# One more gate through half-size products, and a shorter score loop in attention

## The chip, the cores and the metric

The kernel runs on one core of a Trainium2 chip. A core has a matrix engine (TensorE, PE in the profile; its weight loads stand as PEld), a vector engine (VectorE, DVE), an activation engine (ScalarE, ACT), a general engine (GpSimd, POOL) and an engine whose queue issues nearly all transfers (SyncE, SP). They run side by side and wait for each other by semaphores. Matrix products land in PSUM, eight banks of 512 float32 numbers on each of 128 partitions; everything else is held in SBUF. The metric is the time of one execution on the device in microseconds, as a median of runs.

## The reference

One layer on 1024 latent tokens and 256 context tokens of width 1024. A normalised, modulated input `h` goes through one wide projection, whose columns feed two branches and their gates:

```python
pl = project(modulate(x, sh_x, sc_x), w_in[layer])
...
s1 = jnp.einsum('bhqd,bhkd->bhqk', qb1, k1).astype(jnp.float32) * scale
s2 = jnp.einsum('bhqd,bhkd->bhqk', qb2, k2).astype(jnp.float32) * scale
a = jax.nn.softmax(s1, axis=-1) - lam * jax.nn.softmax(s2, axis=-1)
return jnp.einsum('bhqk,bhkv->bhqv', a.astype(v.dtype), v)
...
a = merge_heads(rms_norm(o_gla) * gla_gain) * jax.nn.silu(gla_gate)
b = merge_heads(rms_norm(o_diff) * diff_gain * (1 - lam_init)) * jax.nn.silu(diff_gate)
y = jax.nn.sigmoid(m_gla) * (a @ w_br_gla) + jax.nn.sigmoid(m_diff) * (b @ w_br_diff)
return y @ w_out
```

Branch A is a gated linear attention (`o_gla`); branch B is differential attention over 8 heads: each query has two softmaxes ("components") over 1280 keys, and the second, times a number `lam`, is taken from the first. `m_gla` and `m_diff` are the two merge gates, each a 1024 x 1024 by 1024 x 1024 product of `h` with columns of `w_in`.

## The kernel before

A planner in Python writes the order of every engine's instructions. Each piece of work is a generator with a priority; the `Driver` (lines 46 to 187) keeps an estimated clock for each engine, resumes the generator that is due with the lowest priority number, and adds the instruction's estimated cost. `acq` and `rel` hand out buffers of a tag (line 235: tag, pool, number of buffers), an `Event` passes a dependency on. What comes out is a fixed order for each engine; on the chip an engine waits where an operand is late. All compute instructions are issued at two helper lines: 201 for ACT, DVE and POOL, 349 for matmuls (375 for transposes), so the profile tells them apart by tile names.

Every float32 product is three passes of rounded halves (`mm3`, line 354): high by high, high by low, low by high.

The stages, in order of time:

1. Input, norms, and the products for the linear attention's keys and queries.
2. Groups of paired products (`pairs`, line 1097; `BY7`, line 907): a product of two 2 x 2 block matrices is made with seven half-size products (`p1` to `p7`) and sums of blocks. Four groups so far: the two value projections (five tiles of 128 tokens a half) and the two branch gates (four tiles, `dg` and `gg`). The sums of blocks of `h` (`sums`, line 909) are stored to DRAM once and loaded by each group, 16 loads a group; the sums of the weights are made on DVE (`pair_weights`, line 943).
3. "Late" products (keys and queries of differential attention, six slices of the first merge gate) run on TensorE while the linear attention (`gla_head`, line 1499) goes through all engines.
4. Differential attention: 8 heads x 8 query tiles = 64 tiles of 128 queries.
5. The product of branch B and the output product, again by seven half-size products (`diff`, `phase_c`).

Attention, which the change touches most: `att_scores` (line 1940) makes a tile's scores in one PSUM area `s5` of five banks: 1280 columns of component 0, 1280 of component 1. Bank 2 holds the end of the one and the start of the other, the "tail" (two pieces of 256 columns, `TAIL`). Three tokens guard the area: `s0`, `s1`, and `st` for the shared bank, released after both exponentials. For each tile DVE takes three maxima (`att_max`, line 1991: 1024 columns of component 0, the tail for both, 1024 of component 1), two minima join them (the maxima are negated), and ACT makes two exponentials over 1280 columns that read PSUM and sum as they go (`att_exp`, line 1998). `att_mix` (line 2018) joins the two on DVE: `E0 + cf * E1`. `att_tr` (line 2039) transposes the mix in ten pieces of 128 columns on TensorE, `split2` (line 2120) makes the halves on ACT, POOL and DVE, and `att_av` (line 2068) multiplies by the values, two tiles ("a pair") at a time. `att_fin` (line 2143) normalises a pair's output: copy, transpose, sum of squares, product with the gate from DRAM, power -0.5 on POOL, scaling, transpose back, store.

The order of scores (S), transposes (T) and value products (A) on TensorE is written out by hand (`att_order`, line 1915): scores run three to four tiles ahead of transposes. Whatever TensorE time is left is given to `fill` (line 2194), priority 9, the last of all: half tiles of 24 matmuls. Its list is two slices of the first merge gate, all eight of the second, and eight of `a @ w_br_gla`; slice by slice, halves of tokens in turn. `PACE` (line 2107) holds the i-th half tile back until query tile `1.3 * i` has its scores. PSUM in attention: five banks of scores, two banks `b1` for transposes, value products and the finish, one bank `mb` for the filler.

## Time and profile before

| | |
|---|---|
| time, median of 3 runs (lowest to highest) | 1619.05 us (1618.73 to 1619.51) |
| the profiled execution | span 1614.1 us from the first to the last instruction; its own time isn't given apart from the median, 4.95 us over the span |
| granted TensorE clock, mean | 1.000 |
| busy share of PE, PEld, DVE, ACT, POOL | 99%, 82%, 76%, 52%, 39% |
| DMA | 331.16 MB, mean 205 GB/s |
| attention, first score to last exponential | 898.8 to 1428.6 us |

A row of a group reads: line, engine, operation, output tile <- input tiles, shapes, count | busy microseconds, mean nanoseconds of one | idle time of the engine ahead of them, and who ended it. Matmuls are pipelined: the duration of one is longer than the distance to the next. A row of the timeline has start and length in microseconds, engine, operation, tiles and count, then in brackets the idle time before it. A row of the chain has start, length, engine, output tile and line.

### The profile page before, as it was taken

What the parts mean: (1) busy time and instruction counts of PE and PEld (TensorE: products, weight loads), DVE (VectorE), ACT (ScalarE), POOL (GpSimd) and SP (SyncE); (2) the same over time, 40 slices, a digit from 0 to 9 for tenths busy, and PEclk for the clock granted to TensorE, in tenths of its full rate; (3) what the DMA queues carried; (4) which work ended last, traced back from release to release, by engine and by line L of the source; (5) the groups of instructions that cost most, each with busy time, mean ns of one, the idle gap of its engine ahead of it and who ended that gap; (6) DMA issues with size and microseconds to landing.
All of it is one profiled execution on the core that took longest, in us unless ns stands there. A gap on an engine that the chain in (4) does not pass through costs nothing.

```text
span 1614.1 us, 24349 instructions
## 1 busy us (share of the span) xinstructions
PE 1591.4 (99%) x8229; PEld 1328.1 (82%) x8229; DVE 1224.4 (76%) x2118; ACT 835.7 (52%) x1720; POOL 634.3 (39%) x663
## 2 busy tenths in 40 slices
PE   8999999999999999999999999999999999999999
PEld 3788888888888888888888788888888888888887
DVE  4787945676777779767677688878778888888994
ACT  4776523435343454555535566665665666656331
POOL 1500000001415667535564256656765666560000
PEclk9999999999999999999999999999999999999999
DMA  8576996998878367564645944545587545347662
GB/s 305 201 257 239 329 304 232 344 331 295 278 238 281 116 194 235 167 212 118 189 118 158 253 121 121 151 129 151 150 264 218 159 137 150 111 155 285 204 206 100
DMA packets 259565, 331.16 MB, mean 205 GB/s; under 512 B 22600, under 2 KB 160752, under 8 KB 259440
## 3 DMA queue, kind: packets, MB, share of 16 engines
q1 hardware_dynamic: 259440, 329.60, 63.8%
q8 instruction: 65, 1.06, 0.3%
q14 instruction: 60, 0.49, 0.1%
HBM read 225.20 MB, written 104.33 MB: 204 GB/s over the span
## 4 chain that ended last, share of the span: by engine, by line
PE 89%; DVE 4%; issue 2%; DMA 2%; ACT 1%; POOL 1%; SPq 0%; ACTq 0%; DVEq 0%; POOLq 0%
PE mm L349 30%; PE mb L349 11%; PE s L349 8%; PE mc L349 7%; PE b L349 6%; PE tp L349 5%; PE gt L349 5%; PE b L375 5%; PE go L349 4%; PE gs L349 4%; PE mz L349 2%; PE tp L375 2%; DVE sm L201 1%; POOL at L201 1%; DMA w<-in_w_ada 1%
## 5 line engine op out<-in xcount | busy, mean ns | idle before, releaser
L349 PE MATMUL mm<-w,h 128*128 128x512 f32 x912 | 231.0, 400 | 0.0
L349 PE MATMUL mb<-h,wt 128*128 128x512 f32 x840 | 223.0, 400 | 0.0
L201 DVE TENSOR_REDUCE sm<-s 128x1 f32<-128x1024 f32 (+1 forms) x192 | 193.3, 1037 | 10.7 <-PE s L349 6.6
L201 ACT ACTIVATE e<-s,sm 128x1280 f32<-128x1280 f32 x128 | 169.3, 1329 | 54.4 <-DVE sm L201 51.2
L349 PEld LDWEIGHTS mm<-w,h 128*128 128x128 f32 x912 | 167.4, 188 | 32.8
L201 POOL TENSOR_TENSOR at<-ac,at 128x512 fp32r<-128x512 f32 x128 | 188.2, 1471 | 10.7
L349 PEld LDWEIGHTS mb<-h,wt 128*128 128x128 f32 x840 | 151.4, 188 | 28.6 <-DVE ft L201 0.3
L201 POOL TENSOR_SCALAR at<-ac 128x512 fp32r<-128x512 f32 x128 | 96.9, 757 | 191.0 <-ACT ac L201 190.7
L349 PE MATMUL s<-hk,aq 128*128 128x512 f32 x744 | 169.0, 363 | 1.9 <-ACT e L201 1.8
L349 PE MATMUL mm<-h,w 128*128 128x512 f32 x672 | 168.2, 400 | 1.0 <-DVE h L201 1.0
L349 PEld LDWEIGHTS mm<-h,w 128*128 128x128 f32 x672 | 123.7, 188 | 26.4 <-DVE h L201 1.5
L201 DVE TENSOR_TENSOR w<-raw,w 128x512 fp32r<-128x512 f32 x128 | 96.0, 766 | 54.2 <-ACT w L201 52.0
L349 PEld LDWEIGHTS s<-hk,aq 128*128 128x128 f32 x744 | 117.7, 189 | 18.5 <-ACT e L201 3.6
L349 PE MATMUL b<-at,vv 128*128 128x256 f32 x960 | 130.1, 287 | 1.1 <-ACT ac L201 0.8
L349 PEld LDWEIGHTS b<-at,vv 128*128 128x128 f32 x960 | 119.5, 191 | 2.8 <-ACT ac L201 1.0
L201 ACT ACTIVATE w<-raw 128x512 fp32r<-128x512 f32 x128 | 78.1, 626 | 84.2 <-PE tp L349 23.8
L201 ACT ACTIVATE ac<-b 128x512 f32<-128x512 f32 x122 | 72.5, 598 | 91.8 <-PE b L375 91.7
L201 POOL TENSOR_TENSOR sm<-sm,nhalf 128x2 f32<-128x2 f32 (+2 forms) x94 | 107.7, 1146 | 27.9 <-DVE sm L201 22.7
L201 DVE SCALAR_TENSOR_TENSOR e<-e,sm,e 128x1280 f32<-128x1280 f32 x64 | 117.9, 1842 | 1.0
L349 PE MATMUL mm<-w,g 128*128 128x512 f32 x432 | 105.7, 389 | 0.0
L349 PEld LDWEIGHTS mm<-w,g 128*128 128x128 f32 x432 | 81.1, 188 | 16.9
L375 PE MATMUL b<-ident,e 128*128 128x128 f32 x610 | 92.6, 273 | 1.3 <-ACT ac L201 0.8
(357 smaller groups left out, 3054.2 us busy)
## 6 DMA issues: line engine op xcount, KB each, us to landing
raw<-in_w_in SPq DMA_DIRECT2D x62, 512.0 KB, 4.3
g<-d_s SPq DMA_DIRECT2D x32, 640.0 KB, 6.2
g<-d_s SPq DMA_DIRECT2D x32, 512.0 KB, 5.7
aq<-d_qT SPq DMA_DIRECT2D x124, 128.0 KB, 3.4
d_dv<-pl SPq DMA_DIRECT2D x40, 256.0 KB, 3.9
gv<-d_v SPq DMA_DIRECT2D x40, 256.0 KB, 3.3
d_kT<-pl SPq DMA_DIRECT2D x40, 256.0 KB, 2.8
hk<-d_kT SPq DMA_DIRECT2D x32, 320.0 KB, 5.9
```

The lines of the kernel that those rows point to most:

```text
L201: self.ins = f(out, *args, **kw).ins
L349: self.ins = self.nc.tensor.matmul(out, lhsT, rhs, start=start, stop=stop, skip_group_check=more).ins
L375: self.nc.tensor.transpose(out, src, self.ident[:n, :n])
```

## The change

- The second merge gate (`md`) leaves the filler and becomes the fifth group of paired products, with four tiles. Its output is wanted with channels on the partitions, so the weights are the stationary operand and `h` the moving one, with the roles of the two swapped against the other groups; `out` and `direct` put it through tanh and store it. The filler keeps 10 slices; its pace is 2.4 tiles for a half tile.
- Scores: component 1's turn starts with the tails of both components, once `s1` and `st` are free, and then its 1024 columns. `att_max` is gone: `att_exp` takes one maximum over a component's 1280 columns, and there are no minima.
- `att_mix` of a tile waits until the next tile's second maximum has been issued.
- The bank `mb` is gone; `b1` has three banks, which the filler shares. `mz`, used after attention, has three banks, and the closing products use it where they used `mb`.
- `att_fin`: one product of two columns for the two tiles' scales instead of two; a copy of the transposed output to SBUF, from which the squares are made; sum and scale in one instruction for both tiles; the scaling and the product with the gate in one instruction for each tile.

Two hunks that only open and close the pool of `mb` are left out:

```diff
--- before.py
+++ after.py
@@ -252,11 +252,11 @@
         mm=("psA", 3), tp=("psA", 2), edge=("sbE", 1), gs=("psA1", 1), go=("psA1", 1), gt=("psA1", 1),
-        mb=("psW", 1), s0=("psB", 1), s1=("psB", 1), st=("psB", 1), s5=("psB", 1), b1=("psB1", 2), mc=("psC", 5), mz=("psD", 2),
+        s0=("psB", 1), s1=("psB", 1), st=("psB", 1), s5=("psB", 1), b1=("psB1", 3), mc=("psC", 5), mz=("psD", 3),
     )
...
                  sbA1="right", sbA2="right", sbW="right", sbG="right", sbF="right", sbD="right",
-                 psA="left", psW="left", psB="left", psC="left", psA1="right", psB1="right", psD="right")
+                 psA="left", psB="left", psC="left", psA1="right", psB1="right", psD="right")
     def __init__(self, tc, nc, a, out):
@@ -904,7 +904,8 @@
     NR, NS, TG = 3, 2, 60.0
-    BY7 = (("gv", C_GV), ("dv", C_DV), ("dg", C_DG), ("gg", C_GG))
+    BY7 = (("gv", C_GV), ("dv", C_DV), ("dg", C_DG), ("gg", C_GG), ("md", C_MD))
+    SHORT = ("dg", "gg", "md")
     def sums(self):
@@ -1029,7 +1030,7 @@
                             self.rel(tag, e, 1 + (tag == "pl"))
-                        if (n, k) == ("t4" if g == 3 else "t3", 1):
+                        if (n, k) == ("t3", 1):
                             d.set(ev_win[g])
@@ -1107,7 +1108,7 @@
             for g, (what, _) in enumerate(self.BY7):
-                w = 512 if what in ("dg", "gg") else 640
+                w = 512 if what in self.SHORT else 640
                 for n in self.SUMS:
@@ -1128,6 +1129,8 @@
             h = H[n]
+            if self.BY7[g][0] == "md":
+                return [ev_z[g, h, k].z[:, j] if isinstance(h, str) else self.hx[j][k + h[1]][h[0]] for j in range(2)]
             if isinstance(h, str):
@@ -1136,8 +1139,10 @@
                 yield ev_z[g, H[n], k]
-            sh, sl = left(g, n, k, t)
-            e = self.mm3(pm, sh, sl, *wp[g, W[n], k].w, first, last, True)
+            s, m = left(g, n, k, t), wp[g, W[n], k].w
+            if self.BY7[g][0] == "md":
+                s, m = [x[:, t * P:(t + 1) * P] for x in m], s
+            e = self.mm3(pm, *s, *m, first, last, True)
             if t == nt - 1:
@@ -1146,7 +1151,7 @@
         for g, (what, _) in enumerate(self.BY7):
-            nt = 4 if what in ("dg", "gg") else 5
+            nt = 4 if what in self.SHORT else 5
             A, B, TBt = [None] * 5, [None] * 5, [None] * 5
@@ -1155,6 +1160,11 @@
                 what = self.BY7[g][0]
+                if what == "md":
+                    yield d.on("ACT", x)
+                    self.act.activation(x, x, AF.Tanh, scale=0.5)
+                    self.store([(self.d_m[1][4 * c + t][:, r * 512:(r + 1) * 512], x)], (tag, 1))
+                    return
                 if what in ("dg", "gg"):
@@ -1248,6 +1258,12 @@
         o = self.tok(8 if t == 4 else t)
+        if self.BY7[g][0] == "md":
+            yield from self.acq("p")
+            x = self.t("p", [P, 512])
+            self.rel(tag, self.act.activation(x, pm, AF.Tanh, scale=0.5))
+            self.store([(self.d_m[1][4 + t][:, :512], x)], ("p", 1))
+            return
         if self.BY7[g][0] in ("dg", "gg"):
@@ -1956,56 +1972,46 @@
                     return e
-                u = dict(hd=hd, qt=qt, E=[None, None], mt=self.t("sm", [P, 2]), mx=[self.t("sm", [P, 1]) for _ in range(2)],
-                         z=self.t("sm", [P, 2]), left=2, ev=[Event() for _ in range(3)])
+                if qt % 2 == 0:
+                    zp = self.t("sm", [P, 2, 2])
+                u = dict(hd=hd, qt=qt, E=[None, None], mx=[self.t("sm", [P, 1]) for _ in range(2)],
+                         z=zp[:, qt % 2], zp=zp, left=2)
                 for comp in range(2):
                     yield from self.acq(f"s{comp}")
-                    pm = s5[:, 1536 * comp:1536 * comp + 1024]
-                    if comp == 0:
-                        yield from self.turn("S", 8 * hd + qt, 0)
+                    if comp:
+                        yield from self.acq("st")
+                    yield from self.turn("S", 8 * hd + qt, comp)
                     if self.flush:
                         self.flush(1)
+                    if comp:
+                        for x in range(2):
+                            e = score(s5[:, 1024 + 256 * x:1280 + 256 * x], x, *self.TAIL[x])
+                        d.spawn(self.att_exp(u, 0, s5), On(e, "DVE"), prio=-3)
                     for x, (o, n) in enumerate(self.MAIN[comp]):
-                        e = score(pm[:, x * 512:(x + 1) * 512], comp, o, n)
-                        if x == 0:
-                            yield AtPE(0)
+                        e = score(s5[:, 1536 * comp + 512 * x:1536 * comp + 512 * x + n], comp, o, n)
                     self.passed("S", 8 * hd + qt, comp)
-                    d.spawn(self.att_max(u["ev"][comp], u["mx"][comp], pm, 3 * comp, 3 * comp + 1), On(e, "DVE"), prio=-3)
-                    yield AtPE(0)
-                    if comp == 0:
-                        yield from self.acq("st")
-                        yield from self.turn("S", 8 * hd + qt, 1)
-                        pt = s5[:, 1024:1536].rearrange("p (c k) -> p c k", c=2)
-                        for x in range(2):
-                            e = score(pt[:, x], x, *self.TAIL[x])
-                        d.spawn(self.att_max(u["ev"][2], u["mt"], pt, 2), On(e, "DVE"), prio=-3)
-                    elif qt == 7:
-                        self.rel("kk", e, 2)
-                    d.spawn(self.att_exp(u, comp, s5), On(e, "DVE"), prio=-3)
+                    if comp:
+                        d.spawn(self.att_exp(u, 1, s5), On(e, "DVE"), prio=-3)
+                        if qt == 7:
+                            self.rel("kk", e, 2)
                     yield AtPE(0)
...
                 d.set(self.ev_u[8 * hd + qt])
-    def att_max(self, ev, mx, pm, *banks):
-        self.dve.tensor_reduce(mx, pm, AX.X, ALU.max, negate=True)
-        self.banked(self.dve.ins, "DVE", *banks)
-        self.d.set(ev)
-        return
-        yield
-
     def att_exp(self, u, comp, s5):
         d, mx = self.d, u["mx"][comp]
-        yield u["ev"][2]
-        yield u["ev"][comp]
-        yield d.on("DVE", mx)
-        self.dve.tensor_scalar(mx, mx, u["mt"][:, comp:comp + 1], None, ALU.min)
+        sc = s5[:, T * comp:T * comp + T]
+        self.dve.tensor_reduce(mx, sc, AX.X, ALU.max, negate=True)
+        self.banked(self.dve.ins, "DVE", *range(2 * comp, 2 * comp + 3))
+        if comp:
+            d.set(self.ev_m[8 * u["hd"] + u["qt"]])
         yield self.ev_sb
...
         yield d.on("ACT", mx)
-        e = self.act.activation(E, s5[:, 1280 * comp:1280 * comp + T], AF.Exp, bias=mx, accum_out=u["z"][:, comp:comp + 1])
+        e = self.act.activation(E, sc, AF.Exp, bias=mx, accum_out=u["z"][:, comp:comp + 1])
         self.banked(self.act.ins, "ACT", *range(2 * comp, 2 * comp + 3))
@@ -2020,6 +2026,10 @@
         E, z = u["E"], u["z"]
+        n = 8 * u["hd"] + u["qt"]
+        if n < 63:
+            yield self.ev_m[n + 1]
+        yield On(0, "DVE")
         self.dve.reciprocal(cf, z[:, 1:2])
@@ -2027,7 +2037,7 @@
             e = self.dve.scalar_tensor_tensor(E[0], E[1], cf, E[0], ALU.mult, ALU.add)
-        self.att[u["hd"], u["qt"]] = (E[0], z)
+        self.att[u["hd"], u["qt"]] = (E[0], u["zp"])
         self.rel("e5", e)
@@ -2098,13 +2108,13 @@
                     self.rel("vv", e, 2)
-                d.spawn(self.att_fin(hd, pr, po, [self.att[hd, 2 * pr + x][1] for x in range(2)]), On(e, "ACT"),
+                d.spawn(self.att_fin(hd, pr, po, self.att[hd, 2 * pr][1]), On(e, "ACT"),
                         prio=-5 if hd == 7 and pr > 1 else self.PF)
                 yield AtPE(0)
-    PO, FI = "b1", "mb"
-    PACE = 1.3
+    PO, FI = "b1", "b1"
+    PACE = 2.4
     flush, FG, FN = None, (0,), 2
@@ -2140,48 +2150,44 @@
         return e
-    def att_fin(self, hd, pr, po, zs):
+    def att_fin(self, hd, pr, po, zp):
         nc, d = self.nc, self.d
...
             "(c p) e -> p c e", p=P))
-        ot = self.t("b1k", [P, 256])
-        e = self.act.activation(ot, po, AF.Copy)
+        ot = self.t("b1k", [P, 2, P])
+        e = self.act.activation(ot.rearrange("p x t -> p (x t)"), po, AF.Copy)
         self.rel(self.PO, e)
         z2 = self.t("sm", [P, 2])
-        for x in range(2):
-            self.dve.tensor_scalar(z2[:, x:x + 1], zs[x][:, 0:1], zs[x][:, 0:1], EPS, ALU.mult, ALU.mult)
+        self.dve.scalar_tensor_tensor(z2, zp[:, :, 0], EPS, zp[:, :, 0], ALU.mult, ALU.mult)
         yield AtPE(e)
...
         for x in range(2):
-            e = self.tr(pt[:, x], ot[:, x * P:(x + 1) * P])
+            e = self.tr(pt[:, x], ot[:, x])
+        yield On(e, "ACT")
+        oc = self.t("b1k", [P, 2, P])
+        ss = self.t("sm", [P, 2])
+        self.rel("b1", self.act.activation(oc, pt, AF.Copy))
+        for x in range(2):
+            e = self.act.activation(ot[:, x], oc[:, x], AF.Square, accum_out=ss[:, x:x + 1])
         self.rel("b1k", e)
-        yield On(e, "ACT")
-        oo = self.t("b1k", [P, 2, P])
-        ss = self.t("sm", [P, 2])
+        yield On(e, "DVE")
+        self.dve.scalar_tensor_tensor(ss, ss, 1.0 / P, z2, ALU.mult, ALU.add)
+        yield d.on("POOL", ss)
+        yield On(max(self.pool.tensor_tensor(ss, ss, self.nhalf[:, 0:2], ALU.pow), d.when(g)), "DVE")
         for x in range(2):
-            e = self.act.activation(oo[:, x], pt[:, x], AF.Square, accum_out=ss[:, x:x + 1])
-        yield d.on("DVE", pt, g)
-        e2 = self.dve.tensor_tensor(g, pt, g, ALU.mult)
-        self.rel("b1", max(e, e2))
-        yield On(e, "DVE")
-        for x in range(2):
-            self.dve.tensor_scalar(ss[:, x:x + 1], ss[:, x:x + 1], 1.0 / P, z2[:, x:x + 1], ALU.mult, ALU.add)
-        yield d.on("POOL", ss)
-        yield On(self.pool.tensor_tensor(ss, ss, self.nhalf[:, 0:2], ALU.pow), "DVE")
-        for x in range(2):
-            e = self.dve.tensor_scalar(oo[:, x], g[:, x], ss[:, x:x + 1], None, ALU.mult)
+            e = self.dve.scalar_tensor_tensor(oc[:, x], oc[:, x], ss[:, x:x + 1], g[:, x], ALU.mult, ALU.mult)
         self.rel("b1k", e)
...
         for x in range(2):
-            e = self.tr(pb[:, x], oo[:, x])
+            e = self.tr(pb[:, x], oc[:, x])
         self.rel("b1k", e)
@@ -2195,7 +2201,7 @@
         d, a = self.d, self.a
-        todo = [(0, s, self.win, C_MG + s * P) for s in range(self.fill_from, 16)] + \
+        todo = [(0, s, self.win, C_MG + s * P) for s in range(self.fill_from, 8)] + \
                [(1, s, a["w_br_gla"][0], s * P) for s in range(8)]
@@ -2507,7 +2513,7 @@
             d.set(self.ev_y[dt, c], e)
-        Z = ("mc", "mb", "mz", "mz")
+        Z = ("mc", "mz", "mz", "mz")
         A, B = [None] * 4, [None] * 4
@@ -2601,6 +2607,7 @@
             d.spawn(g(), prio=-1)
+        self.ev_m = [Event() for _ in range(64)]
         self.att_order()
@@ -2737,7 +2744,7 @@
         def stream():
-            Z = ("mz", "mz", "mc", "mb")
+            Z = ("mz", "mz", "mc", "mz")
             A, B = [None] * 4, [None] * 4
```

4 lines of the change are left out of this document (2 added, 2 removed).

## The prediction

> **What bounds the kernel now.** I read the head of the page first, then the chain that ended last, then the busy times by stretch.
>
> ```profile
> span 1614.1 us, 24349 instructions
> PE 1591.4 (99%) x8229; PEld 1328.1 (82%) x8229; DVE 1224.4 (76%) x2118; ACT 835.7 (52%) x1720; POOL 634.3 (39%) x663
> PE 89%; DVE 4%; issue 2%; DMA 2%; ACT 1%; POOL 1%; SPq 0%; ACTq 0%; DVEq 0%; POOLq 0%
> ...
> 320.00:360.00 40.00, 40.00 (x178) 33.13 (x177) 28.44 (x45) 15.41 (x26) 0.00 (x0) 1.00 0.97 355
> 360.00:400.00 40.00, 39.28 (x174) 32.19 (x173) 28.59 (x41) 22.39 (x38) 6.22 (x4) 1.00 0.77 269
> ...
> 898.80:1428.60 529.80, 524.22 (x3189) 454.83 (x3190) 441.04 (x805) 322.07 (x651) 323.26 (x287) 1.00 0.55 159
> ```
>
> In the stretches the columns are length, then PE, PEld, DVE, ACT, POOL busy, granted clock, DMA share, GB/s. TensorE is nearly always busy. The 4.95 us between this span and the median of 1619.05 us lie outside the span; I take them as unchanged and make the sum on the median. The first two stretches lie in the groups of paired products: PE stays full even where DMA is 97% busy, and at a seam between groups it loses 0.72 us. The last stretch is attention, first score to last exponential: 64 query tiles in 529.8 us, 8.28 us each, of which DVE is busy 6.89 (83%), ACT 5.03, POOL 5.05.
>
> What TensorE does there, by the chain and the timeline:
>
> ```profile
> 1016.78 2.32 PE s L349 x12
> 1019.54 2.15 PE b L349 x18
> 1022.13 1.44 PE b L349 x12
> ...
> 1442.86 1.25 PE L375 MATMUL mc<-ident,e 128*128 128x128 f32 x10
> 1443.87 5.06 PE L349 MATMUL mc<-h,wt 128*128 128x512 f32 x21
> 1448.78 0.38 PE L375 MATMUL b<-ident,b1k 128*128 128x128 f32 x2
> ...
> 1457.66 0.39 PE L349 MATMUL mc<-xa,hk 128*128 128x512 f32 x1
> ...
> 1471.53 2.88 PE L349 MATMUL mb<-h,wt 128*128 128x512 f32 x12
> 1474.25 5.60 PE L349 MATMUL mz<-h,wt 128*128 128x512 f32 x24
> ```
>
> One tile needs 12 score matmuls (2.32 us), ten transposes (1443.87 - 1442.86 = 1.01), half of a pair's 30 value matmuls ((2.15 + 1.44)/2 = 1.80) and two small transposes (0.2): 5.33 us. The other 2.9 us of the 8.28 are filler: matmuls of gates and of the first branch, which run where attention leaves PE free. So PE is full, but attention's own loop does not run at PE's speed; filler hides that. Why the loop takes 8.28 us stands in the timeline of one tile:
>
> ```profile
> 1104.57 1.33 ACT L201 ACTIVATE e<-s,sm 128x1280 f32<-128x1280 f32 x1 [1.26 <-DVE sm L201]
> ...
> 1105.80 0.19 ACT L201 ACTIVATION_READ_ACCUMULATOR e<-s,sm 128x1 f32 x1
> 1105.89 1.32 ACT L201 ACTIVATE e<-s,sm 128x1280 f32<-128x1280 f32 x1
> ...
> 1107.33 0.16 DVE L201 RECIPROCAL sm<-sm 128x1 f32<-128x1 f32 x1 [0.60 <-ACT e L201]
> 1107.53 0.28 DVE L201 TENSOR_SCALAR sm<-sm,sm,nlam 128x1 f32<-128x1 f32 x1
> ...
> 1109.10 2.10 DVE L201 SCALAR_TENSOR_TENSOR e<-e,sm,e 128x1280 f32<-128x1280 f32 x1
> ...
> 1111.46 1.81 DVE L201 TENSOR_REDUCE sm<-s 128x2 f32<-128x512 f32 x2
> 1113.19 0.33 DVE L201 TENSOR_SCALAR sm<-sm,sm 128x1 f32<-128x1 f32 x2
> ...
> 1113.42 1.34 ACT L201 ACTIVATE e<-s,sm 128x1280 f32<-128x1280 f32 x1
> ```
>
> Both exponentials wait for the shared tail maximum, and the mix of the tile before (2.10 us) stands ahead of it on DVE; from exponential to exponential it is 8.85 us.
>
> **The change part by part.** *The gate moved into the groups.* Out of attention go 8 slices x 2 halves x 8 blocks x 3 passes = 384 matmuls at 0.234 us ((1448.78 - 1443.87)/21), 89.8 us. Into the groups go 7 products x 4 blocks x 4 tiles x 3 passes = 336 at 0.227 us ((1474.25 - 1471.53)/12), 76.2 us, and a seam: nothing to 0.72, I take 0.4. Net -13.2 us; the low bound is the 48 matmuls alone, -10.9.
>
> ```profile
> L201 DVE TENSOR_TENSOR w<-raw,w 128x512 fp32r<-128x512 f32 x128 | 96.0, 766 | 54.2 <-ACT w L201 52.0 <-PE gs L349 1.0 <-PE tp L349 0.9
> g<-d_s SPq DMA_DIRECT2D x32, 512.0 KB, 5.7
> L201 DVE TENSOR_TENSOR wt<-raw,wt 128x1024 fp32r<-128x1024 f32 x17 | 22.7, 1335 | 0.9 <-ACT wt L201 0.9
> L201 ACT ACTIVATE wt<-raw 128x1024 fp32r<-128x1024 f32 x17 | 18.2, 1070 | 0.0
> L201 ACT ACTIVATE ft<-mb 128x512 f32<-128x512 f32 x20 | 12.1, 606 | 4.3 <-PE mb L349 3.6 <-DMA aq<-d_qT 0.7
> ```
>
> The new group's 28 weight splits, 16 combinations and 12 additions, all at DVE's 0.766, are 43 us in 76, under PE. Its weight loads and the stores of the gate move with it; new on SP's queue are 16 loads of 512 KB (two short groups have 32), 8.4 MB. The stretch at 97% DMA hides them; uncovered, 8.4 MB at its 355 GB/s are 24 us, the worst end. I take 0. They stand ahead of the late jobs' weights, as the fourth group's do now.
>
> *What attention then needs.* Filler falls from 864 to 480 matmuls, 112.3 us or 1.75 a tile: PE 7.08 us a tile. That is the pace if PE stays the bound. The other engines have to come under it:
>
> ```profile
> L201 DVE TENSOR_REDUCE sm<-s 128x1 f32<-128x1024 f32 x128 | 155.7, 1216 | 10.7 <-PE s L349 6.6 <-ACT e L201 3.6
> L201 DVE TENSOR_REDUCE sm<-s 128x2 f32<-128x512 f32 x64 | 43.5, 680 | 0.0
> L201 DVE TENSOR_SCALAR sm<-sm,sm 128x1 f32<-128x1 f32 x192 | 32.8, 206 | 0.7
> L201 DVE TENSOR_SCALAR sm<-sm 128x1 f32<-128x1 f32 x64 | 10.4, 203 | 0.0
> L201 DVE TENSOR_TENSOR b1k<-b,b1k 128x256 f32<-128x256 f32 x32 | 13.2, 413 | 0.0
> L201 DVE TENSOR_SCALAR b1k<-b1k,sm 128x128 f32<-128x128 f32 x64 | 26.6, 457 | 30.3 <-POOL sm L201 30.3
> L201 DVE SCALAR_TENSOR_TENSOR e<-e,sm,e 128x1280 f32<-128x1280 f32 x64 | 117.9, 1842 | 1.0
> L201 ACT ACTIVATE b1k<-b 128x256 f32<-128x256 f32 x64 | 24.8, 388 | 30.8 <-PE b L375 25.2 <-PE b L349 5.2
> ```
>
> A maximum over 1280 is not in the trace; by the slope between the two reductions, 1.216 + 256 x (1.216 - 0.680)/512 = 1.48 us, from 1.22 (no longer than 1024) to 1.90 (their sum). 128 of them are 190 us for 199.2: -9.3. The 128 minima go (two thirds of 32.8): -21.9. Half of the two small scalings in the finish go: -5.5 and -5.2. The product with the gate goes: -13.2; the last scaling becomes a product of two tensors, 0.21 to 0.84 us by halving or doubling its row; I keep its own 0.42. Eight weight splits of 1.335 go: -10.7. DVE 441 - 66 = 375 us, 5.86 a tile, which is 83% of 7.08: the share it reaches now. ACT loses 8 splits of 1.07 and 16 tanh of 0.606, and gains 32 copies of 0.388: under 5 us a tile. POOL stays at 5.05.
>
> *The loop.* Each instruction on `s5` waits for the other engines' last one on a bank of its own (`banked`). The two components share bank 2, and the second maximum is emitted before the first exponential, which so waits for both, as in the timeline above. From one release of the bank to the next: four tail matmuls (about 0.6 with their end), two maxima (2.96), two exponentials (2.66) and the sum's end (0.19): 6.4 us, and if all of the mix (1.84, and 0.16 + 0.28 for its coefficient) stays in the way, 8.7. Could the first exponential run beside the second maximum, it would be 5.1. The mix is now emitted behind the next tile's second maximum, and from there to the next first maximum DVE has 3.45 us (exponentials, sum, tails) for 2.28 of mix and about 0.6 of the rest (5.86 - 2.96 - 2.28). So it should fit; I take 6.6, near to 6.4. That is under 7.08 by half a microsecond, and PE binds, but narrowly. Behind the waiting mix on DVE stand only splits and finishes; its own transposes come three to four tiles later by the written order.
>
> *Small edits.* The filler's pacing allows 24 matmuls per 2.4 tiles, 2.3 us a tile; the first four tiles have scores only, so about 3 us a tile are free and 0.7 stay empty: +3 us (0 to 6). The three shared banks equal two and one whenever filler holds one: 0. The last finish has one copy of 0.388 more, and the second tile of the closing product waits for attention's banks, 12 matmuls or 2.7 us of lost cover: 0 to 3, I take 1. PE and the loop are so close that one will now and then wait for the other: in the trace PE waited 2.0 us in all for exponentials; 0 to 6, I take 1 more.
>
> Sum: 1619.05 - 13.2 + 3 + 1 + 1 = 1611 us.
>
> A row speaks against the finish's new product:
>
> ```profile
> L201 DVE TENSOR_TENSOR pl<-tp,pl 128x512 fp32r<-128x512 f32 x51 | 34.6, 685 | 26.5 <-ACT pl L201 26.5
> ...
> L201 DVE TENSOR_TENSOR hk<-raw,hk 128x512 fp32r<-128x512 f32 x4 | 5.2, 1350 | 0.0
> ```
>
> The same subtraction takes 685 ns with one operand in PSUM and 1350 with both in SBUF late in attention, where POOL is busy. The rule for this in the Trainium skill, page "SBUF — State Buffer", section "Who interferes with whom", is that a VectorE instruction with two SBUF inputs contends with a GpSimd instruction that reads SBUF, and one with a single SBUF input outside the two-port modes doesn't; the two rows agree. By it the new product, both operands in SBUF, pays what the old one from PSUM did not; by my row it pays nothing new.
>
> **The rivals.** *The loop becomes the bound (0.17, slower).* DVE takes its work in one order; if a split, a finish or the end of a mix stands ahead of the first maximum by 0.8 us on average, a tile takes 7.4 us, filler runs out, and PE stands at the tails for 64 x (7.4 - 7.08) = 20 us: 1631. It is a loss from 7.08 + 8/64 = 7.2 us a tile on. For it: the bank shared by both components puts maxima and exponentials in a row, and the margin is small. Against it: today's 8.28 is the old chain with the mix in it.
>
> *Products of two SBUF tensors collide with POOL (0.09, slower).* A two-tensor mix of 1280 takes 1.84 where a reduction of that length is 1.48; if the new products and the mix, now beside a POOL that is busy 71% and not 61% of the time, lose as much again, 0.36 a tile more on DVE makes 6.22, at the share of 83% a tile of 7.49: 64 x 0.41 = 26 us, 1637. Against it: the scaling that is replaced has already 0.42 us for 128 elements. It is what the Trainium skill's rule named above would do here.
>
> *The loop eats just the gain (0.17, no difference).* A tile of about 7.2 us, 1619: 0.6 us over my 6.6 is all that it takes.
>
> *More than the sum (0.10, faster).* The shorter loop also saves what PE loses now: 864 filler matmuls at 0.234 and 64 x 5.33 are 543 us, of 529.8 and the 29 from 1428.6 to the closing product at 1457.7; if the 15 between halve, it is 1611 - 7.5, about 1603.
>
> **How the numbers follow.** PE stays the bound at 0.47: 1611 us, its own range 1605 to 1616 by the bounds of seam, start and end. With the last rival, faster has 0.57; no difference 0.17; slower 0.26. No change means within 0.2%, 3.2 us, about what a measurement of this kernel can tell. The range runs from 1600 to 1634: it takes in the last rival's centre, all of the third and the first's centre; left out are the collision and the outer halves of its neighbours.
>
> **What would show it.** Right: 336 more matmuls at 0.227 us ahead of attention and attention beginning some 77 us later; a pace near 7.1 us a tile with filler until the last tile; a maximum of about 1.48 us with the mix behind the next tile's second one; DVE near 83% there. Wrong: PE waiting at score tails for the exponential, filler ending tiles before the last exponential, a last scaling over 0.6 us, or PE idle in the fifth group.

## The result, and the profile after

| | before | after |
|---|---|---|
| time, median of 4 runs each (lowest to highest) | 1618.89 us (1617.72 to 1619.51) | 1721.11 us (1717.12 to 1721.55) |
| ratio, 95% interval | | 1.063 (1.0615 to 1.0645) |
| profiled span | 1614.1 us | 1715.4 us |
| first score | 898.8 us | 986.1 us |
| first score to last exponential | 529.8 us | 542.4 us |
| from there to the end | 185.5 us | 186.9 us |

The change makes the kernel 6% slower; the prediction was 1611. The 101.3 us between the spans are 87.3 ahead of attention, 12.6 in it and 1.4 behind it. Ahead of attention 76.6 had been forecast. So 11 us of the miss lie ahead of attention. The rest lies in attention and the filler left over behind it: together they should have become 86 us shorter (384 matmuls out, 4 us of small losses back), and they became 14 us longer.

The head of the page after, its chain by engines, and three stretches (columns as in the prediction):

```profile
span 1715.4 us, 24242 instructions
PE 1622.2 (95%) x8181; PEld 1336.4 (78%) x8181; DVE 1209.3 (70%) x1878; ACT 862.1 (50%) x1784; POOL 601.5 (35%) x663
PE 78%; DVE 9%; issue 5%; ACT 5%; DMA 3%; SPq 0%; POOL 0%; DVEq 0%; ACTq 0%; POOLq 0%
...
440.00:480.00 40.00, 38.67 (x171) 31.54 (x169) 30.91 (x45) 17.56 (x31) 6.15 (x4) 1.00 0.63 204
480.00:520.00 40.00, 37.03 (x155) 30.10 (x156) 25.32 (x33) 13.52 (x23) 16.20 (x12) 0.96 0.84 286
...
986.10:1528.50 542.40, 475.00 (x2808) 397.83 (x2809) 382.99 (x514) 312.06 (x652) 294.55 (x287) 0.95 0.47 137
```

TensorE's share of the span falls from 99% to 95%, DVE's share of the chain rises from 4% to 9%. In attention TensorE was busy 524 of 530 us, and is now busy 475 of 542, at a granted clock of 0.95. DVE is busy 382.99 us there, not 441.04: its work became smaller by 58 us, nearly the 66 that were forecast. It does less and the loop takes longer; so neither PE nor DVE binds by the amount of its work. What binds are waits. First those of the two loops, before and then after (columns: who waits for whom, us in total, times, longest; the window is first score to last exponential):

```profile
ACT e L201 <- DVE sm L201: 51.2, 48, 3.4
DVE sm L201 <- PE s L349: 6.6, 10, 2.8
PEld s L349 <- ACT e L201: 4.3, 6, 1.8
```

```profile
ACT e L201 <- DVE sm L201: 165.9, 64, 4.9
DVE sm L201 <- PE s L349: 93.6, 34, 6.4
DVE at L201 <- ACT at L201: 48.1, 30, 2.3
PEld s L349 <- ACT e L201: 40.1, 46, 4.0
PE s L349 <- ACT e L201: 23.0, 24, 3.6
```

The exponential now waits for a maximum at every tile, 2.6 us each time; the maxima wait for scores, and the scores for the exponential. All three are one ring. The timeline of the changed kernel shows it for two tiles:

```profile
1270.87 1.65 PE L349 MATMUL s<-hk,aq 128*128 128x256 f32 x8
1271.70 2.89 DVE L201 TENSOR_REDUCE sm<-s 128x1 f32<-128x1280 f32 x2 [1.77 <-PE s L349]
...
1274.63 1.33 ACT L201 ACTIVATE e<-s,sm 128x1280 f32<-128x1280 f32 x1 [2.31 <-DVE sm L201]
...
1275.95 0.59 ACT L201 ACTIVATE ac<-b 128x512 f32<-128x512 f32 x1
1276.42 1.33 ACT L201 ACTIVATE e<-s,sm 128x1280 f32<-128x1280 f32 x1
...
1278.64 0.42 DVE L201 TENSOR_TENSOR at<-b,at 128x256 fp32r<-128x256 f32 x1 [1.68 <-ACT at L201]
1278.98 2.88 DVE L201 TENSOR_REDUCE sm<-s 128x1 f32<-128x1280 f32 x2
...
1281.89 1.33 ACT L201 ACTIVATE e<-s,sm 128x1280 f32<-128x1280 f32 x1 [3.29 <-DVE sm L201]
...
1284.27 1.68 PE L349 MATMUL b<-at,vv 128*128 128x256 f32 x12
...
1287.07 1.65 PE L349 MATMUL s<-hk,aq 128*128 128x256 f32 x8
...
1287.90 2.89 DVE L201 TENSOR_REDUCE sm<-s 128x1 f32<-128x1280 f32 x2 [2.47 <-PE s L349]
1290.82 1.33 ACT L201 ACTIVATE e<-s,sm 128x1280 f32<-128x1280 f32 x1 [2.31 <-DVE sm L201]
```

Tails, two maxima in a row, then the first exponential, a copy for the splits, the second exponential, tails: the order that the prediction wrote down. It gave 6.4 us for it. Here it takes 7.26 in the first tile (1281.89 - 1274.63) and 8.93 in the second (1290.82 - 1281.89). What the sum lacked stands in between: a copy on ACT between the exponentials (0.59), a split on DVE that waits for ACT ahead of the maxima (1278.64, 1.68 of waiting), and in every other tile the tails stand behind the value products in TensorE's written order (1284.27).

### The profile page after: what moved, and what is told of

Its sections match the earlier page's. It is cut to its first block, busy times and chain, and to the rows that moved or that the text cites. A ratio compares the mean times of both kernels' runs of the same rounds, so it can differ in the third digit from the quotient of the medians.

```text
span 1715.4 us, 24242 instructions
## 1 busy us (share of the span) xinstructions
PE 1622.2 (95%) x8181; PEld 1336.4 (78%) x8181; DVE 1209.3 (70%) x1878; ACT 862.1 (50%) x1784; POOL 601.5 (35%) x663
## 4 chain that ended last, share of the span: by engine, by line
PE 78%; DVE 9%; issue 5%; ACT 5%; DMA 3%; SPq 0%; POOL 0%; DVEq 0%; ACTq 0%; POOLq 0%
PE mm L349 30%; PE b L349 8%; PE s L349 7%; PE mc L349 7%; PE tp L349 6%; DVE sm L201 6%; PE gt L349 5%; PE gs L349 4%; PE go L349 4%; PE b L375 3%; PE mz L349 3%; ACT e L201 2%; PE tp L375 2%; ACT ac L201 1%; DMA w<-in_w_ada 1%
## 5 line engine op out<-in xcount | busy, mean ns | idle before, releaser
L201 ACT ACTIVATE e<-s,sm 128x1280 f32<-128x1280 f32 x128 | 170.1, 1330 | 165.9 <-DVE sm L201 165.9
L201 DVE TENSOR_REDUCE sm<-s 128x1 f32<-128x1280 f32 x128 | 185.1, 1484 | 94.8 <-PE s L349 93.6
L349 PE MATMUL s<-hk,aq 128*128 128x512 f32 x744 | 189.4, 398 | 23.2 <-ACT e L201 23.0
L201 POOL TENSOR_TENSOR at<-ac,at 128x512 fp32r<-128x512 f32 x128 | 172.4, 1347 | 10.7
L349 PEld LDWEIGHTS s<-hk,aq 128*128 128x128 f32 x744 | 126.9, 210 | 53.7 <-ACT e L201 40.1
L201 DVE TENSOR_TENSOR w<-raw,w 128x512 fp32r<-128x512 f32 x144 | 105.5, 753 | 67.4 <-ACT w L201 65.5
L201 ACT ACTIVATE w<-raw 128x512 fp32r<-128x512 f32 x144 | 87.2, 626 | 99.1 <-PE tp L349 23.8
L349 PE MATMUL b<-h,wt 128*128 128x512 f32 x432 | 114.8, 401 | 0.0
L375 PEld LDWEIGHTS b<-ident,e 128*128 128x128 f32 x610 | 73.9, 143 | 52.1 <-issue 26.9
L201 DVE SCALAR_TENSOR_TENSOR e<-e,sm,e 128x1280 f32<-128x1280 f32 x64 | 101.8, 1590 | 2.0
L201 ACT ACTIVATE p<-mm 128x512 f32<-128x512 f32 (+1 forms) x113 | 65.7, 586 | 68.1 <-PE mm L349 53.3
```

What stands on the lines that cost most here:

```text
L201: self.ins = f(out, *args, **kw).ins
L349: self.ins = self.nc.tensor.matmul(out, lhsT, rhs, start=start, stop=stop, skip_group_check=more).ins
L375: self.nc.tensor.transpose(out, src, self.ident[:n, :n])
```

## The experiments

Two theories at the start. *Filler*: attention's loop takes about 8 us whatever stands between, and filler only used its gaps, so taking 384 matmuls out saves little and the fifth group is paid in full. *The single maximum*: the new order of tails, maxima and exponentials is what makes the loop long. All runs in one table; the ratio is to the kernel before as it was run beside each (medians from 1616.8 to 1618.9 us), the last column is the number of filler matmuls between first score and last exponential, a tile is the stage by 64:

| kernel | us | ratio to before, 95% | first score | attention | a tile | filler |
|---|---|---|---|---|---|---|
| before | 1618.9 | | 898.8 | 529.8 | 8.28 | 797 |
| after | 1721.1 | 1.0615 to 1.0645 | 986.1 | 542.4 | 8.48 | 416 |
| group alone | 1693.6 | 1.0429 to 1.0499 | 984.5 | 512.3 | 8.00 | 480 |
| attention alone | 1728.6 | 1.0644 to 1.0716 | 900.4 | 538.6 | 8.42 | 410 |
| three maxima | 1689.3 | 1.0407 to 1.0468 | 986.2 | 511.3 | 7.99 | 480 |
| planner knows | 1720.6 | 1.0600 to 1.0662 | 986.7 | 541.6 | 8.46 | 480 |
| mix at once | 1737.7 | 1.0719 to 1.0762 | 985.3 | 549.1 | 8.58 | 344 |
| own banks | 1683.3 | 1.0383 to 1.0424 | 987.2 | 502.2 | 7.85 | 480 |
| bank for filler | 1726.9 | 1.0652 to 1.0694 | 988.2 | 548.3 | 8.57 | 475 |
| mix and finish on before | 1649.2 | 1.0181 to 1.0230 | 901.2 | 503.6 | 7.87 | 562 |
| mix alone on before | 1641.8 | 1.0136 to 1.0170 | 900.1 | 516.7 | 8.07 | 626 |
| two slices moved | 1688.2 | 1.0420 to 1.0462 | 978.1 | 514.2 | 8.03 | 576 |
| five slices moved | 1679.7 | 1.0371 to 1.0402 | 952.8 | 532.9 | 8.33 | 720 |
| scores first | 1739.1 | 1.0723 to 1.0785 | 989.5 | 559.0 | 8.73 | 480 |

**The group alone.** The kernel before with the fifth group and the slower pace; attention is the old one.

```diff
-    BY7 = (("gv", C_GV), ("dv", C_DV), ("dg", C_DG), ("gg", C_GG))
+    BY7 = (("gv", C_GV), ("dv", C_DV), ("dg", C_DG), ("gg", C_GG), ("md", C_MD))
-    PACE = 1.3
+    PACE = 2.4
-        todo = [(0, s, self.win, C_MG + s * P) for s in range(self.fill_from, 16)] + \
+        todo = [(0, s, self.win, C_MG + s * P) for s in range(self.fill_from, 8)] + \
```

> The kernel before with one part of the change: the second merge gate as fifth group of paired products, and the filler's pace of 2.4; attention with three maxima, the mix at once, the filler's own bank and the old finish. Theory 'bank': attention was slowed by the new score loop (one maximum over the bank that both components share), not by the loss of filler. Then this kernel's attention follows its shorter list of TensorE work, near 7.1 us a tile, and the whole is 1605 to 1625 us. Rival 'filler': the loop of attention was 8.28 us a tile in either form and filler only hid it. Then attention keeps some 530 us, the group's 76 us come on top less the 15 us of filler that ran after the last exponential, and the whole is 1670 to 1685 us.

1693.6 us: 75 of the 102 us come from here, with nothing of attention's code changed; that is 9 us above the range of the rival "filler" and far above that of the other theory. Attention is 17.5 us shorter for 384 matmuls less (90 us by their own length), and the time behind it is 7.5 us longer (193.0 against 185.5). Its two parts, with filler and after the last of it at 1369.4 (the stretches, and the count of exponentials, two a tile, in each):

```profile
984.50:1369.40 384.90, 364.94 (x2190) 311.78 (x2191) 319.46 (x586) 222.17 (x454) 238.24 (x207) 0.99 0.58 168
1369.40:1496.80 127.40, 108.95 (x678) 88.40 (x677) 106.63 (x210) 81.34 (x171) 90.28 (x80) 0.96 0.31 88
```

```profile
L201 ACT ACTIVATE e<-s,sm 128x1280 f32<-128x1280 f32 x94 | 124.4, 1328 | 65.5 <-DVE sm L201 63.4 <-PE b L375 1.9
L201 ACT ACTIVATE e<-s,sm 128x1280 f32<-128x1280 f32 x35 | 46.4, 1328 | 12.2 <-DVE sm L201 12.2
```

47 tiles in 384.9 us are 8.19 a tile; 17.5 tiles in 127.4 are 7.28, with no filler at all. The old loop takes 7.28 us by itself, though TensorE's own work in a tile is 5.33. The 480 filler matmuls lengthened it by 47 x (8.19 - 7.28) = 43 us, 0.09 us each, where each takes 0.234. Filler was costed at its length, and in the loop it costs little more than a third of it. The place in the stage isn't the reason: in the kernel before, which has filler to the end, the last 16 tiles take 8.25 us each (1296.6 to 1428.7), here 7.39 (1378.5 to 1496.8). The theory of the filler holds in its mechanism; its number, a loop of 8.28 us in either form, doesn't.

**Attention alone.** The changed kernel with the gate back in the filler at its old pace; two buffers of the closing product are taken only once the filler's operands are loaded.

```diff
-        todo = [(0, s, self.win, C_MG + s * P) for s in range(self.fill_from, 8)] + \
+        todo = [(0, s, self.win, C_MG + s * P) for s in range(self.fill_from, 16)] + \
-    PACE = 2.4
+    PACE = 1.3
```

> The changed kernel with the second merge gate back in the filler (four groups, pace 1.3, 18 slices); the new score loop, the later mix, the three shared banks and the new finish stay. Two buffer tags of the closing product are given out only after the filler's operands are loaded, which the order needs. Theory 'bank': the new loop costs 8.5 us a tile by itself; the filler fills its gaps, but not wholly: 1630 to 1660 us. Rival 'filler': a loop of 8.3 to 8.5 us a tile is what attention has anyway, so this is the kernel before: 1615 to 1625 us.

1728.6 us, far above both forecasts (at most 1660): the new attention by itself is 110 us slower than the old one. Its stage is 538.6 us, and only 410 of 864 filler matmuls found a place in it (797 before); the rest follow behind, where the time from last exponential to end is 286 us instead of 185: 100 of the 110 us. The new loop is as long as in the changed kernel with the same filler inside, so the shortage of filler isn't what makes it long.

**Three maxima.** The changed kernel with scores, three maxima and two minima as before; group, later mix, banks and finish stay changed.

```diff
+                    d.spawn(self.att_max(u["ev"][comp], u["mx"][comp], pm, 3 * comp, 3 * comp + 1), On(e, "DVE"), prio=-3)
...
-        self.dve.tensor_reduce(mx, sc, AX.X, ALU.max, negate=True)
+        self.dve.tensor_scalar(mx, mx, u["mt"][:, comp:comp + 1], None, ALU.min)
```

> The changed kernel with the old scores and maxima: component 0's 1024 columns, the tails, component 1's 1024 columns, three maxima and two minima; the fifth group, the later mix, the three shared banks and the new finish stay. Theory 'bank': the loop gets most of its loss back; 1610 to 1650 us, TensorE waiting under 50 us in attention. Rival 'filler': no change from the changed kernel, 1700 to 1725 us.

1689.3 us, between the two forecasts: the single maximum costs 31.8. The stage and the two waits of this kernel:

```profile
986.20:1497.50 511.30, 464.96 (x2866) 403.34 (x2866) 426.95 (x709) 313.99 (x651) 325.21 (x286) 0.98 0.52 148
```

```profile
DVE sm L201 <- PE s L349: 70.3, 35, 4.6
ACT e L201 <- DVE sm L201: 63.4, 50, 4.5
```

DVE has 44 us more to do (426.95 against 382.99), and the stage is 31 us shorter. ACT's wait for the maxima falls from 165.9 to 63.4. So the edit that saved DVE time put it on the ring: with three maxima the long one of the first component is done before the shared bank is full, and only the short one over the tails stands between bank and exponential; with one each, both whole maxima do. Against the group alone, the later mix, the three shared banks and the new finish together gave 4.3 us, and the intervals of the two ratios overlap, so that this may be nothing.

**Planner knows.** The planner's estimate counts the whole-component maxima and exponentials on the shared bank too.

```diff
+        tails = [self.key(x)[:-1] + "t" for x in shared if getattr(x, "tensor", x).name.startswith("s5") and x.free_size() > 512]
...
-        for x in shared:
+        for k in [self.key(x) for x in shared] + tails:
```

> The changed kernel, but the planner is told that a maximum or an exponential over 1280 columns also touches the shared tail bank (on the chip it does: semaphores make it wait); only the order of the instructions changes. Theory 'bank' in the form that the order is made for a loop that the chip can't run (the planner lets the first exponential run beside the second maximum): 1650 to 1695 us, with fewer long waits of TensorE between transposes. If only the chip's chain itself counts and the order does not: 1710 to 1725 us. Rival 'filler': 1710 to 1725 us.

1720.6, the changed kernel's time, though all 480 filler matmuls now stand inside attention (416 in the changed kernel). A bad order from this wrong estimate is not the cause.

**Mix at once.** The changed kernel without the wait in `att_mix`.

```diff
-        n = 8 * u["hd"] + u["qt"]
-        if n < 63:
-            yield self.ev_m[n + 1]
-        yield On(0, "DVE")
```

> The changed kernel with one edit undone: the mix of a tile no longer waits for the next tile's second maximum and is emitted on DVE as soon as its exponentials are planned. Theory 'chain' (the loop tails, two maxima, two exponentials sets the pace): 2.0 us of mix and coefficient now stand between the last exponential and the next first maximum, of which some 0.6 us are hidden by the tail matmuls; up to 64 x 1.4 = 90 us more, about 1780 us, at least 1740. Rival 'transposes late' (the postponed mix holds up transposes and value products, and these the scores behind them in TensorE's written order): it gets faster, about 1700. Rival 'neither': 1721 within 5.

1737.7, 16.6 us slower than with the later mix and just under the 1740 given as the least. The waits in its attention:

```profile
ACT e L201 <- DVE sm L201: 136.9, 64, 5.4
DVE sm L201 <- ACT e L201: 96.8, 50, 3.3
PEld s L349 <- ACT e L201: 70.0, 56, 4.0
```

DVE now stands at the mix and waits for the exponential 96.8 us, in front of the maxima. Within this loop the later mix does what it says, but the price of undoing it is a fifth of the 90 us that were given as the most: the mix mostly fills time in which the maxima would have waited for scores (that wait falls from 93.6 us to 10.8). In the profiled executions attention itself is only 6.7 us longer; 16.4 us lie behind it (203.3 against 186.9), where 72 more filler matmuls were left over.

**Own banks.** Each maximum over the component's own 1024 columns; in a second hunk the scores are scaled by 0.015625 instead of 0.125, so the output is another one.

```diff
-        self.dve.tensor_reduce(mx, sc, AX.X, ALU.max, negate=True)
-        self.banked(self.dve.ins, "DVE", *range(2 * comp, 2 * comp + 3))
+        self.dve.tensor_reduce(mx, s5[:, 1536 * comp:1536 * comp + 1024], AX.X, ALU.max, negate=True)
+        self.banked(self.dve.ins, "DVE", 3 * comp, 3 * comp + 1)
```

> The changed kernel, but each component's maximum is taken over the 1024 columns of its own two banks alone; the 256 columns in the shared bank are left out of the maximum, and the scores are made smaller by a constant so that the exponentials stay finite (so the output is another one; every other instruction is as it was). Theory 'shared bank': the first maximum no longer waits for the tails, and so not for the exponentials of the tile before, and the first exponential no longer waits for the second maximum: about one us a tile, 1655 us, under the 1689 of the run with three maxima. Rival 'only the length': each maximum is 0.26 us shorter (1.22 for 1.48), 64 x 0.52 = 33 us, about 1688. Rival 'not the loop': 1721 within 5.

1683.3, nearest to "only the length" (1688), and 28 us from what the shared bank was said to give. The waits in its attention:

```profile
DVE sm L201 <- PE s L349: 88.5, 55, 5.8
ACT e L201 <- DVE sm L201: 65.9, 37, 2.6
```

ACT waits for maxima as little as with three of them (65.9, 63.4), and both kernels have nearly the same pace, 7.85 and 7.99 a tile. Length alone doesn't explain both, since three maxima are longer than one. What they have in common is that no whole maximum stands between the full bank and the first exponential. Taking that away wins back 32 to 38 us and no more: it leads back to the 8.00 us a tile of the group alone. What makes those 8 us these runs don't isolate, nor how much of the 38 us comes from the shorter maxima and how much from the bank.

**Bank for filler.** The changed kernel with a bank of its own for the filler and two for the rest.

```diff
-    PO, FI = "b1", "b1"
+    PO, FI = "b1", "mb"
```

> The changed kernel with one edit undone: the filler has its own PSUM bank again, and transposes, value products and the finish have two. Theory (the three shared banks are worth nothing here): 1721 within 6. Rival 'the filler takes the bank that a transpose needs': faster, 1700 or less.

1726.9, 5.8 us slower, just within the 6 of the forecast: three shared banks are worth little.

**Mix and finish, and mix alone, on the kernel before.** Later mix and new finish in the old kernel; then the mix alone:

```diff
+        n = 8 * u["hd"] + u["qt"]
+        if n < 63:
+            yield self.ev_m[n + 1]
+        yield On(0, "DVE")
         self.dve.reciprocal(cf, z[:, 1:2])
```

> The kernel before with two of the small edits alone: the mix waits for the next tile's second maximum, and the new finish; the three maxima, the gate in the filler, its pace and the bank for the filler stay. Theory (attention of before is full of filler, TensorE is busy 99%, and DVE's shorter work is worth little): 1617, 1610 to 1622. Rival 'later mix pays by itself': under 1605, 0.3 us a tile. Rival 'the later mix holds up the transposes': over 1630.

> The kernel before with the later mix alone (the mix waits for the next tile's second maximum); finish, maxima, filler, pace and banks as before. The run with later mix and new finish took 1649, its attention 26 us shorter and 235 filler matmuls left over behind it. If the later mix makes attention's loop shorter and so leaves the filler less room in the written order: 1640 to 1650 with over 150 filler matmuls left over. If the new finish does (its products of two tensors took 0.92 us there, 0.43 in the changed kernel): 1619 within 6, and nearly all the filler inside.

1649.2 and 1641.8. The time is near the last rival's of the first expectation, and its reason is not: attention is 26 and 13 us shorter, and the kernel 31 and 25 us slower than the kernel before as run beside it. The groups of the filler's matmuls in the stage, with both edits and then with the mix alone:

```profile
L349 PE MATMUL mb<-h,wt 128*128 128x512 f32 x562 | 154.1, 405 | 1.9 <-DVE wt L201 1.5 <-DVE ft L201 0.3
```

```profile
L349 PE MATMUL mb<-h,wt 128*128 128x512 f32 x626 | 170.9, 401 | 0.7 <-DVE ft L201 0.7
```

235 and 171 filler matmuls fewer than before's 797, all of them done later: 55 and 40 us by 0.234, and the time from last exponential to end grew by 56 and 38. By 0.09 us each they explain 21 of the 26 us and 15 of the 13 in attention too. So the later mix hardly changes the loop here; it changes the planner's order so that less filler is put into it, and filler outside costs its full length. The expectation of 1640 to 1650 with over 150 matmuls left over held. The finish costs 6 to 7 us on top. The group of its new scaling on DVE, first with mix and finish on before, then in the changed kernel:

```profile
L201 DVE SCALAR_TENSOR_TENSOR b1k<-b1k,sm,b1k 128x128 f32<-128x128 f32 x64 | 52.7, 863 | 9.5 <-POOL sm L201 7.0 <-DMA b1k<-d_dg 2.1 <-DMA d_m<-ft 0.4
```

```profile
L201 DVE SCALAR_TENSOR_TENSOR b1k<-b1k,sm,b1k 128x128 f32<-128x128 f32 x64 | 30.7, 520 | 0.8 <-DMA aq<-d_qT 0.5 <-POOL sm L201 0.3
```

**Slices moved back.** The group alone, with two and with five of the six slices of the first merge gate that ran beside the linear attention moved into the filler.

```diff
-        NM = 2
+        NM = 1
-                                            self.NS if m else 4))
-        self.fill_from = 4 + self.NS
+                                            1))
+        self.fill_from = 1
-    PACE = 2.4
+    PACE = 2.0
```

> As the run with five slices moved, with two: filler 576 matmuls, pace 2.2. Theory 'filler is nearly free': 96 x (0.234 - 0.07) = 16 us, 1678. Rival 'TensorE binds everywhere': 1694 within 5. Rival 'the linear attention's own chain binds': the same 1678 here, and nothing more from the other three slices.

> The kernel before with the fifth group alone, as in the run of the group, but five of the six slices of the first merge gate that run beside the linear attention are moved into the filler of attention (filler 720 matmuls instead of 480, its pace 2.0 tiles instead of 2.4). Theory 'filler is nearly free' (attention's own chain sets about 7.4 us a tile without any filler and 8.3 with it, and TensorE stands empty when filler runs out): 240 x 0.234 = 56 us leave the time ahead of attention, and attention grows by 240 x 0.07 = 17 us (0.07: 18 us for the 384 that the group took out, with some to spare): 1694 - 56 + 17 = 1655, 1640 to 1665. Rival 'TensorE binds everywhere': work is only moved, 1694 within 5. Rival 'the linear attention's own chain binds once these products are gone': attention begins less than 30 us earlier, 1680 or more. To beat the kernel before it would have to come under 1616, which only the first theory with a full attention stage (1694 less 86 empty us) comes near.

1688.2 and 1679.7 from 1693.6; neither is a time that a theory gave (1679.7 lies just under the rival's 1680). In attention the theory of the filler holds: 96 more filler matmuls lengthen it by 2 us, 240 by 21, 0.02 and 0.09 each. Ahead of it, it doesn't: the five slices are 56 us, and the first score comes only 32 us earlier, just over the 30 that the rival of the linear attention had set; with two slices it is 6.4 for 22.5 us moved. The two stretches ahead of the first score with five slices moved:

```profile
880.00:920.00 40.00, 35.49 (x179) 29.50 (x178) 30.15 (x64) 21.02 (x63) 23.08 (x30) 0.96 0.39 123
920.00:960.00 40.00, 28.41 (x138) 22.85 (x137) 24.81 (x50) 20.68 (x60) 10.42 (x20) 0.91 0.55 156
```

TensorE stands at the end of the linear attention; that its own chain is then the longer one fits this and wasn't tested further. So the gap that the second gate leaves in attention can't be refilled from there in full, and no version was found that beats the kernel before.

**Scores first.** The changed kernel with the second tile's scores ahead of the second half of the value products.

```diff
-            order += T(o) + S(o + lead) + [t[0], a[0], t[1], a[1], s[0], t[2], s[1]]
+            order += T(o) + S(o + lead) + [t[0], a[0], s[0], t[1], s[1], a[1], t[2]]
```

> The changed kernel with another written order on TensorE alone: the second tile of a pair has its scores ahead of the first tile's last transposes and the second half of the value products, not behind them (s0 after a0, s1 after t1). In the trace of the changed kernel every other tile's tails stand behind 12 value matmuls, and those tiles take 8.7 to 11.2 us against 7.3 for the others. Theory 'the written order, made for separate maxima, adds to the chain': the long tiles come down to about 8, 30 x 1.7 = 50 us, 1670. Rival 'the chain tails, two maxima, two exponentials alone': every tile stays at 7.3 or more and the stall moves to the value products; 1700 to 1725. Rival 'worse': value products late, finishes late, over 1730.

1739.1, worse. Moving the scores up doesn't shorten the loop (8.73 us a tile), the wait only changes places: the maxima wait 65.6 us for scores instead of 93.6, and the exponential 190.9 for maxima instead of 165.9.

## Why the prediction was wrong

- *"Filler hides that."* Right, and read from the right rows: TensorE's own 5.33 us a tile, and a loop that doesn't run at PE's speed. The next step didn't use it. If the loop is longer than PE's own work, filler costs only what it adds to the loop, and taking it out gives back only that. It was costed at 384 x 0.234 = 89.8 us; in the run of the group alone attention gives back 17.5.
- *"PE 7.08 us a tile ... I take 6.6 [for the loop] ... PE binds, but narrowly."* This is the step that failed: attention was given TensorE's pace of 7.08, with a loop of 6.6 under it. The loop took 8.48, within the bounds of 6.4 and 8.7 but near the end that I did not take. 64 x (8.48 - 7.08) = 90 us, nearly all of the 110 us between 1611 and 1721. The new loop makes the smaller part of it. The group alone, with the old maxima, is 83 us over 1611 already, 9 of them ahead of attention; attention's own edits add 27.5. There TensorE's 7.08 us of work and a loop of 7.28 us without filler gave 8.00 a tile: the sum took the greater of two paces as the pace, and here the filler in the ring came on top of it in part. For the new loop the term was built as a chain of the instructions that I had on my list; ACT's copy between the exponentials, the split ahead of the maxima and the value products ahead of the tails were not on it. It also stood beside a measured 8.28 for the old chain, which was put down to the mix alone; without any filler that loop takes 7.28.
- *DVE at 5.86 us a tile and 83%.* The work was right: 382.99 / 64 = 5.98. The share was not: 71%. Less work on an engine in a ring is no shorter ring; three maxima with 44 us more of DVE were 31 us faster.
- *The maximum of 1280 at 1.48 us.* Right to the digit, and the mix lies behind the next tile's second maximum, as forecast. In the changed kernel:

```profile
L201 DVE TENSOR_REDUCE sm<-s 128x1 f32<-128x1280 f32 x128 | 185.1, 1484 | 94.8 <-PE s L349 93.6
...
L201 DVE SCALAR_TENSOR_TENSOR e<-e,sm,e 128x1280 f32<-128x1280 f32 x64 | 101.8, 1590 | 2.0
```

- *The group, 76.2 us and a seam of 0.4.* Right for the group itself: its matmuls fill 515.66 to 591.83 us, 76.2 us, without a pause (second line below). Yet the first score is 87.3 us later, 11 more than that. In the fourth group, just ahead, TensorE stands 4.0 us for a load of that group's sums (first line), and the clock is at half behind it for 3.4 us; from 420 us to the end of that group 6.0 us are lost. The prediction had put what the loads might leave uncovered at 0. Another 2 us are lost before 420 us and 3 behind the fifth group. Why the load came late wasn't isolated.

```profile
482.67 0.96 PE L349 MATMUL gt<-w,g 128*128 128x512 f32 x3 [4.00 <-DMA g<-d_s]
...
515.66:591.83 76.17, 76.17 (x338) 63.06 (x337) 40.46 (x59) 32.59 (x57) 6.21 (x6) 1.00 0.59 191
```

- *The rival "the loop becomes the bound"* was the right mechanism with the wrong size: 7.4 a tile for 8.48. Its place was right too, TensorE at the scores (weight loads there waited 40.1 us for the exponential). Filler didn't run out, though: 64 of its 480 matmuls were left over behind attention. The cause was given as stray work ahead of the first maximum, which no run isolates; what the runs isolate is the whole maximum between the shared bank and the first exponential, 32 to 38 us.
- *The collision with POOL* didn't come about: the mix became shorter, 1.84 to 1.59 us, and the scaling takes 0.52. With POOL busy 323 of 504 us (mix and finish on before) the same scaling takes 0.86, so the price exists. POOL's share alone doesn't set it: with three maxima POOL is as busy (325 of 511 us), and the scaling takes 0.65. That POOL is the reason wasn't isolated.
- *Small edits.* The end was right within its range (1.4 us), and the banks, put at 0, are worth 5.8. The pacing, 0 to 6 us, was sized as if unplaced filler cost its length inside attention; the runs on the kernel before show that the cost comes when filler is left over behind attention.

What stays open: what makes up the 7.28 us of the old loop without filler, where no engine is busy more than 86% (PE, 108.95 of 127.40; DVE, 106.63), and how the 32 us of the single maximum divide between the first maximum waiting for the tails and the first exponential waiting for the second maximum.

## What to carry to other kernels

An engine at 99% can be full of work that only fills gaps. Before work is taken off it, ask what the stage would take without it: find a stretch where the filler has run out, and cost filler at the difference of the two paces, not at its length. And in a ring through three engines count what stands between two hand-overs; splitting a reduction so that its long part runs before the last operand is there can beat the cheaper single one.

## What the runs showed of the hardware

The granted clock fell by itself when TensorE paused: 1.00 over the old attention, 0.95 over the new one; in the group alone 0.99 with filler and 0.96 without; 0.91 at the end of the linear attention with five slices moved. Three stretches of the changed kernel show a single step (the clock is the third number from the end), and the line below them the longest pause in the first:

```profile
1255.10:1258.51 3.41, 1.45 (x11) 0.99 (x9) 3.37 (x7) 1.14 (x1) 0.64 (x1) 1.00 0.23 77
1258.51:1261.92 3.41, 3.08 (x9) 2.45 (x10) 1.19 (x3) 2.84 (x7) 2.54 (x4) 0.50 0.43 126
1261.92:1265.34 3.42, 3.42 (x24) 3.06 (x24) 3.42 (x3) 0.53 (x1) 2.55 (x3) 1.00 0.53 163
...
1257.81 0.41 PE L375 MATMUL b<-ident,e 128*128 128x128 f32 x2 [1.67 <-DVE sm L201]
```

TensorE is busy for 1.45 of 3.41 us, and then its clock is at half for 3.41 us. In the new attention this happens 13 times (11 times for 3.41 us, twice for 6.83), each time behind a stretch of 3.41 us in which TensorE was busy 23 to 50%; of the stretches that left the clock at 1.00 one had 42%, all others 51% or more. In the old attention it doesn't happen. It may be that filler holds the clock up, since it fills such pauses.

The Trainium skill, page "TensorE: Matmul & The Clock Gate", section "Part 1: The HAM clock gate (the "warmup" mystery)", says that the clock is halved after an idle window of about 3.4 us and comes back after one of work. The length of the stretches agrees with it, but here a pause of 1.67 us in a stretch that was 43% busy was enough.

The 51 us at half the clock in the new attention can cost at most 26 us, an estimate from these stretches. They are hardly what makes the new loop long: the runs "planner knows" and "bank for filler" have a mean clock of 0.97 and 0.98 there, and with 64 and 59 more filler matmuls inside their stages take 541.6 and 548.3 us. How much of the 102 us the clock makes can't be told more closely from these runs.
